# Fifteen small loads of 1 to 15 partitions behind the third load of a streaming log-sum-exp

## The chip, the cores and the metric

The kernel runs on one core of a Trainium2 chip. A core has a matrix engine (PE), a vector engine (DVE), a scalar engine (ACT), a general engine (POOL), a sequencer that issues transfers (SP), and 16 DMA engines that move data between the chip's memory (HBM) and the core's own memory (SBUF, 128 partitions). The metric is the device time of one execution in microseconds. Before the change its median is 161.55 us over two runs (161.54 and 161.56).

## The reference

The input is 32 x 512 rows of 1024 float32 numbers, 64 MiB in all. Each row gives one number, the logarithm of the sum of the exponentials of its elements, made safe by taking the row's maximum out first:

```python
max_x = np.max(x, axis=-1, keepdims=True)
return (max_x.squeeze(-1) + np.log(np.sum(np.exp(x - max_x), axis=-1))).astype(np.float32)
```

The input is drawn from a standard normal distribution, so the output is 16384 float32 numbers, 64 KiB.

## The kernel before

The 16384 rows are laid over 128 partitions, 128 rows on each. The rows stream through `ring`, a buffer of 48 rows (192 KiB) in each partition. Eighteen loads bring them in, all issued by SP in program order. The list `LOADS` gives each one's size in rows for each partition, from 16 at the start to 0.47 at the end, and what is done with the rows. Three loads of 16 rows fill the ring; a fourth begins again at its start, and the function `load` (lines 134 to 141) makes SP wait until the engine that used that place last has counted up its semaphore. The first load is moved ahead of the program's opening barrier by `start_early`. Each load has a semaphore of its own (`landed[i]`), which its transfer raises by 16 when all has arrived.

ACT waits for a load to land and replaces its elements by their exponentials in place, without the maximum (line 228). The sums over rows are made by DVE over whole rows (line 239), or by POOL, which adds the two halves of a row (line 233), and DVE over the halves (line 171), or by DVE with an operation that adds halves and sums in one (line 249). The very last row comes in two pieces whose sums ACT makes itself (line 202). Two logarithms on ACT (lines 268 and 281, with line 279 for the rows in between) and two stores on SP (lines 276 and 285) give the result.

Since the exponentials are taken without the maximum, a check runs beside the work: DVE marks sums that lie outside safe limits, PE adds the marks up, and line 308 makes a truth value of them. If it were false, the branch from line 310 on would compute everything again in the safe form; with this input it is not taken. At the end SP waits until the other engines have passed (line 365) and the first store has landed (line 366), clears the semaphores from `landed[0]` up to, but without, `stored` (line 367), and waits for the second store (line 369).

Nothing plans the order of the work: the program is written out, each engine follows its own list, and counters (`Counted`) carry the waits. SP's list in the first part is thus load 1, load 2, load 3, then a wait for DVE's sum over load 1, then load 4, and so on. All of SP's transfers use one hardware queue, whose work the 16 DMA engines do.

Of the kernel before, what the change touches and what calls it, by code (L numbers as in the profile page):

```python
# [15 lines left out]
RING = 48  # L16
B = 16
LATE = 119

# [31 lines left out]
def kernel(  # L53
# [5 lines left out]
    nc = tc.nc  # L59
# [11 lines left out]
    x_flat = x.flatten_outer_dims()  # L71
# [12 lines left out]
    def source(e0, size):  # L84
        assert e0 >= W * d or e0 + size <= W * d
        return x_rest[:, e0 - W * d : e0 - W * d + size] if e0 >= W * d else x_rows[:, e0 : e0 + size]
# [8 lines left out]
    def sbuf(name, cols, dtype=fp32, rows=P):  # L95
        return nc.alloc_sbuf_tensor(name, [rows, cols], dtype).ap()

    ring = sbuf("ring", RING * d)
    sumexp = sbuf("sumexp", NC)
    res = sbuf("res", NC)  # L100
    clamped = sbuf("clamped", NC)
# [18 lines left out]
    done = nc.alloc_semaphore("done")  # L120
    again = nc.alloc_semaphore("again")
    ready = nc.alloc_semaphore("ready")
    stored = nc.alloc_semaphore("stored")

    nc.scalar.preload_act_table_set("natural_log_exp_and_others")  # L125
# [8 lines left out]
    def load(i, here, done_before, size):  # L134
        for a, b, who, at in users:
            if a < here + size and b > here:
                sp.wait(who, at)
        users[:] = [u for u in users if not (u[0] < here + size and u[1] > here)]
        return nc.sync.dma_start(
            out=ring[:, here : here + size], in_=source(done_before, size)  # L140
        ).then_inc(landed[i], 16)

    def check_early():
        dve.wait(act, summed_by_act)
        dve.wait(dve, dve.n)
        dve.did(nc.vector.tensor_scalar(  # L146
            out=clamped[:, 0:LATE], in0=sumexp[:, 0:LATE],
            scalar1=LOW, scalar2=HIGH, op0=ALU.max, op1=ALU.min,
        ))
        dve.wait(dve, dve.n)  # L150
        dve.did(nc.vector.scalar_tensor_tensor(  # L151
            out=clamped[:, 0:LATE], in0=clamped[:, 0:LATE], scalar=0.0, in1=sumexp[:, 0:LATE],
            op0=ALU.bypass, op1=ALU.not_equal, accum_out=bad[:, 0:1],
        ))
        pe.wait(dve, dve.n)
        pe.did(nc.tensor.matmul(count, lhsT=bad[:, 0:1], rhs=far, start=True, stop=False))  # L156

    def add_up(c, who, **kw):
        pe.wait(*who)
        return pe.did(nc.tensor.matmul(count, lhsT=ones, rhs=sumexp[:, c : c + 1], **kw))  # L160
# [3 lines left out]
    def reduce_folded():  # L164

        nonlocal early_sum
        while folded:
            c0, s0, p0, n0 = folded.pop(0)
            halves = ring[:, p0 : p0 + s0 * d].rearrange("p (c d) -> p c d", d=d)[:, :, 0:H]
            dve.wait(pool, n0)  # L170
            at = dve.did(nc.vector.reduce_sum(  # L171
                out=sumexp[:, c0 : c0 + s0], in_=halves, axis=AX.X
            ))
            users.append((p0, p0 + s0 * d, dve, at))
            if c0 < W:
                early_sum = at
# [9 lines left out]
    for i, (size, ops) in enumerate(loads):  # L186
        if here + size > RING * d:
            assert here == p
            p = here = 0
        if any(q < here + size and q + t * d > here for _, t, q, _ in folded):  # L190
            reduce_folded()
        dma = load(i, here, done_before, size)
        first_load = first_load or dma.ins
        end = here + size
        done_before += size
        act.wait(landed[i], 16)
        for k, (how, s) in enumerate(ops):
            rows = ring[:, p : p + s * d].rearrange("p (c d) -> p c d", d=d)
            if how in "YZ":

                assert c == LAST and (how == "Z" or here == p)
                at = act.did(nc.scalar.activation(  # L202
                    out=last_exp[:, here - p : end - p], in_=ring[:, here:end], func=AF.Exp,
                    accum_out=first_sum if how == "Y" else last_sum,
                ))
                if how == "Z":
                    last_piece = ring[:, here:end]
                here = end
                if how == "Y":
                    nc.vector.addr_align(128, offset=0, max_nops=0)  # L210
                    dve.wait(act, at)
                    first_piece = dve.did(nc.vector.tensor_copy(out=sumexp[:, LAST:NC], in_=first_sum))  # L212
                summed_by_act = at
            elif how == "A":
                assert here == p
                v = ring[:, p : p + d]
                at = act.did(nc.scalar.activation(
                    out=v, in_=v, func=AF.Exp, accum_out=sumexp[:, c : c + 1]
                ))
                here += d  # L220
                users.append((p, p + d, act, at))
                summed_by_act = at
                who = (act, at)
            else:

                upto = end if k + 1 == len(ops) and c + s < LAST else p + s * d
                v = ring[:, here:upto]
                at = act.did(nc.scalar.activation(out=v, in_=v, func=AF.Exp))  # L228
                here = upto
            if how == "F":  # L230
                reduce_folded()
                pool.wait(act, at)
                at = pool.did(nc.gpsimd.tensor_tensor(  # L233
                    out=rows[:, :, 0:H], in0=rows[:, :, 0:H], in1=rows[:, :, H:d], op=ALU.add
                ))
                folded.append((c, s, p, at))
            elif how == "R":
                dve.wait(act, at)
                who = (dve, dve.did(nc.vector.reduce_sum(  # L239
                    out=sumexp[:, c : c + s], in_=rows, axis=AX.X  # L240
                )))
                users.append((p, p + s * d, *who))
            elif how == "T":
                if c >= W:
                    reduce_folded()
                dve.wait(act, at)
                for r in range(s):
                    lo = rows[:, r, 0:H]
                    who = (dve, dve.did(nc.vector.scalar_tensor_tensor(  # L249
                        out=lo, in0=lo, scalar=1.0, in1=rows[:, r, H:d],  # L250
                        op0=ALU.mult, op1=ALU.add, accum_out=sumexp[:, c + r : c + r + 1],
                    )))
                    users.append((p + r * d, p + (r + 1) * d, *who))
                    if c + r >= LATE:
                        add_up(c + r, who, start=False, stop=False)
            if how == "A" and c >= LATE:
                add_up(c, who, start=False, stop=False)
            if how in "RT":
                if c < W:
                    early_sum = dve.n  # L260
                reduce_folded()
            c += s
            p += s * d
            if c == LATE:

                act.wait(dve, early_sum)
                act.wait(act, early_act)
                ln_early = act.did(nc.scalar.activation(  # L268
                    out=res[:, 0:W], in_=sumexp[:, 0:W], func=AF.Ln
                ))  # L270
                check_early()
            if c <= W:
                early_act = summed_by_act
        assert here == end
# [7 lines left out]
        out=res[:, LAST:NC], in_=last_sum, func=AF.Ln, bias=sumexp[:, LAST:NC]  # L282
# [7 lines left out]
    dve.did(nc.vector.scalar_tensor_tensor(  # L290
        out=clamped[:, LATE:NC], in0=sumexp[:, LATE:NC], scalar=LOW,
        in1=sumexp[:, LATE:NC], op0=ALU.max, op1=ALU.not_equal, accum_out=bad[:, 1:2],
# [9 lines left out]
        out=over[:, 0:half], in0=last_piece[:, 0:half], scalar=CEILING,  # L302
# [3 lines left out]
    at = pe.did(nc.tensor.matmul(count, lhsT=bad[:, 2:3], rhs=steep, start=False, stop=True))  # L306
    dve.wait(pe, at)
    at = dve.did(nc.vector.tensor_scalar(out=fine, in0=count, scalar1=HIGH, scalar2=None, op0=ALU.is_lt))  # L308
# [10 lines left out]
    with nc.If(all_fine < 1):  # L319
# [5 lines left out]
        for c0 in range(0, NC, RING):  # L325
# [6 lines left out]
            for c1, c2 in ((c0, edge), (edge, c0 + s)):  # L332
                if c1 == c2:
                    continue
                nc.scalar.dma_start(
                    out=ring[:, (c1 - c0) * d : (c2 - c0) * d],
                    in_=source(c1 * d, (c2 - c1) * d),
# [4 lines left out]
                out=neg, in_=v, op=ALU.max, axis=AX.X, negate=True  # L342
# [3 lines left out]
                out=v, in0=v, in1=neg[:, :, None].to_broadcast([P, s, d])  # L346
# [5 lines left out]
                out=sumexp[:, c0 : c0 + s], in_=v, axis=AX.X  # L352
# [11 lines left out]
    nc.scalar.sem_inc(done, 1)  # L364
    nc.sync.wait_ge(done, 2)
    nc.sync.wait_ge(sp.sem, 16)
    nc.sync.sem_clear(range(landed[0].num, stored.num))
    kind = dict(sync_type="semaphore", id=stored.num, ant_name="stored")
    nc.sync.add_instruction(mybir.InstEventSemaphore(
# [53 lines left out]
```

## Time and profile before

| | |
|---|---|
| median of 2 runs | 161.55 us |
| the profiled execution, from first to last instruction (its span) | 160.4 us |
| median less that span | 1.2 us |
| ACT busy, DVE busy, POOL busy | 114.5, 114.3, 37.3 us |
| moved by DMA | 67.18 MB in 2881 packets, 419 GB/s over the span |
| transfers | 18 loads and 2 stores, all issued by SP |

The profile is one execution. Its page gives each engine's busy time, the span cut into 40 slices with a digit for the busy share of each (9 means 90% or more), the DMA queues with packets and bytes, and the chain of work that ended last, followed back from the last instruction. Further views group instructions by line, give each stretch of time its busy sums, and list who waited for whom. "SPq" is SP's list of transfers. The time that is put down to issuing a transfer is SP's own; the time to landing runs from there to the last rise of the transfer's semaphore. Times within the execution count from its first instruction.

### The profile page before, as it was taken

The page shows a single profiled execution, that of the slowest core. Times are in us where ns is not written, and L with a number is a line of the kernel's source. Part 1 is how long each engine was busy: PE and PEld are TensorE (multiplying, and loading weights), DVE is VectorE, ACT ScalarE, POOL GpSimd, SP SyncE. Part 2 cuts the span into 40 slices and gives each one's busy share as a digit, 9 for nine tenths or more (in the row PEclk, how much of TensorE's full clock was granted, in tenths as well). Part 3 has the DMA queues.
Part 4 walks back from the last instruction along what each step waited for, and adds up shares of the span by engine and source line. Part 5 has one row for each costly group of instructions (what it writes and reads, how often), then busy time and mean ns, then how long its engine had stood idle before and what let it go on. Part 6 is the DMA issues. An engine that isn't in the chain of part 4 may idle for free.

```text
span 160.4 us, 219 instructions
## 1 busy us (share of the span) xinstructions
PE 2.2 (1%) x26; PEld 1.1 (1%) x26; DVE 114.3 (71%) x59; ACT 114.5 (71%) x31; POOL 37.3 (23%) x11
## 2 busy tenths in 40 slices
PE   0000000000000000000000000000000000000022
PEld 0000000000000000000000000000000000000011
DVE  0000000009999499994999859959999999999996
ACT  3000059990699708995099949991999989799996
POOL 0000000000000000000000994690004969891000
DMA  7996996996996996996999999999999999999992
GB/s 262 523 523 262 523 523 262 523 507 278 523 490 294 523 490 294 523 490 294 482 441 441 441 425 409 409 409 480 432 395 417 450 416 398 448 411 424 412 413 95
DMA packets 2881, 67.18 MB, mean 419 GB/s; under 512 B 576, under 2 KB 704, under 8 KB 1344
## 3 DMA queue, kind: packets, MB, share of 16 engines
q1 hardware_dynamic: 2880, 67.18, 97.7%
q14 instruction: 1, 0.01, 0.0%
HBM read 67.11 MB, written 0.07 MB: 419 GB/s over the span
## 4 chain that ended last, share of the span: by engine, by line
DMA 52%; ACT 28%; DVE 19%; issue 1%; PE 0%
DMA ring<-in_x_dram 52%; ACT ring L228 27%; DVE sumexp L239 15%; DVE sumexp L171 2%; DVE ring L249 1%; DVE over L301 0%; PE count L306 0%; ACT res L268 0%; DVE clamped L290 0%; DVE fine L308 0%; DVE sumexp L212 0%
## 5 line engine op out<-in xcount | busy, mean ns | idle before, releaser
L228 ACT ACTIVATE ring<-ring 128x16384 f32<-128x16384 f32 (+16 forms) x23 | 111.7, 4908 | 43.0 <-DMA ring<-in_x_dram 43.0
L239 DVE TENSOR_REDUCE sumexp<-ring 128x16 f32<-128x16384 f32 (+4 forms) x9 | 85.6, 9513 | 42.7 <-ACT ring L228 42.7
L233 POOL TENSOR_TENSOR ring<-ring 128x3072 f32<-128x3072 f32 (+3 forms) x7 | 37.1, 5313 | 107.3 <-ACT ring L228 107.3
L171 DVE TENSOR_REDUCE sumexp<-ring 128x6 f32<-128x3072 f32 (+3 forms) x7 | 18.4, 2656 | 0.0
L249 DVE SCALAR_TENSOR_TENSOR ring<-ring 128x512 f32<-128x512 f32 x15 | 9.6, 687 | 0.4 <-ACT ring L228 0.4
L125 ACT ACT_TABLE_LOAD x1 | 1.3, 1283 | 1.4 <-PEq L62 1.4
L156 PE MATMUL count<-far,bad 128*1 128x1 f32 x2 | 0.2, 164 | 153.2 <-DVE clamped L151 153.2
L160 PE MATMUL count<-sumexp,ones 128*1 128x1 f32 x18 | 1.6, 164 | 3.6 <-DVE ring L249 3.6
L249 DVE DVE_READ_ACCUMULATOR ring<-ring 128x1 f32 x15 | 1.2, 82 | 0.0
L202 ACT ACTIVATE last_exp<-ring 128x544 f32<-128x544 f32 (+1 forms) x2 | 1.2, 584 | 0.0
L126 DVE MEMSET ones<- 128x1 f32 x1 | 0.1, 59 | 1.5 <-PEq L62 1.5
L156 PEld LDWEIGHTS count<-far,bad 128*1 128x1 f32 x2 | 0.1, 80 | 153.2 <-DVE clamped L151 153.2
L160 PEld LDWEIGHTS count<-sumexp,ones 128*1 128x1 f32 x18 | 0.8, 80 | 4.5 <-DVE ring L249 4.5
L301 DVE SCALAR_TENSOR_TENSOR over<-ring 128x240 f32<-128x240 f32 x1 | 0.4, 404 | 0.0
L308 DVE TENSOR_SCALAR fine<-count 1x1 int32<-1x1 f32 x1 | 0.1, 147 | 0.3 <-PE count L306 0.3
L151 DVE SCALAR_TENSOR_TENSOR clamped<-clamped,sumexp 128x119 f32<-128x119 f32 x1 | 0.3, 283 | 0.0
L268 ACT ACTIVATE res<-sumexp 128x112 f32<-128x112 f32 x1 | 0.3, 279 | 0.0
L281 ACT ACTIVATE res<-last_sum,sumexp 128x1 f32<-128x1 f32 x1 | 0.3, 261 | 0.0
L202 ACT ACTIVATION_READ_ACCUMULATOR last_exp<-ring 128x1 f32 x2 | 0.3, 126 | 0.0
L146 DVE TENSOR_SCALAR clamped<-sumexp 128x119 f32<-128x119 f32 x1 | 0.2, 221 | 0.0
L279 ACT ACTIVATE res<-sumexp 128x15 f32<-128x15 f32 x1 | 0.2, 209 | 0.0
L290 DVE SCALAR_TENSOR_TENSOR clamped<-sumexp 128x9 f32<-128x9 f32 x1 | 0.2, 169 | 0.0
(17 smaller groups left out, 1.8 us busy)
## 6 DMA issues: line engine op xcount, KB each, us to landing
ring<-in_x_dram SPq DMA_DIRECT2D x1, 6912.0 KB, 23.9
ring<-in_x_dram SPq DMA_DIRECT2D x1, 6400.0 KB, 19.7
ring<-in_x_dram SPq DMA_DIRECT2D x1, 4608.0 KB, 15.9
ring<-in_x_dram SPq DMA_DIRECT2D x1, 3584.0 KB, 24.0
ring<-in_x_dram SPq DMA_DIRECT2D x1, 3072.0 KB, 19.1
ring<-in_x_dram SPq DMA_DIRECT2D x1, 2288.0 KB, 24.1
ring<-in_x_dram SPq DMA_DIRECT2D x1, 1664.0 KB, 20.9
ring<-in_x_dram SPq DMA_DIRECT2D x1, 1264.0 KB, 23.6
```

The source lines that it names most:

```text
L125: nc.scalar.preload_act_table_set("natural_log_exp_and_others")
L151: dve.did(nc.vector.scalar_tensor_tensor(out=clamped[:, 0:LATE], in0=clamped[:, 0:LATE], scalar=0.0, in1=sumexp[:, 0:LATE], op0=ALU.bypass ...
L156: pe.did(nc.tensor.matmul(count, lhsT=bad[:, 0:1], rhs=far, start=True, stop=False))
L160: return pe.did(nc.tensor.matmul(count, lhsT=ones, rhs=sumexp[:, c : c + 1], **kw))
L171: at = dve.did(nc.vector.reduce_sum(out=sumexp[:, c0 : c0 + s0], in_=halves, axis=AX.X))
L202: at = act.did(nc.scalar.activation(out=last_exp[:, here - p : end - p], in_=ring[:, here:end], func=AF.Exp, accum_out=first_sum if how == ...
L228: at = act.did(nc.scalar.activation(out=v, in_=v, func=AF.Exp))
L233: at = pool.did(nc.gpsimd.tensor_tensor(out=rows[:, :, 0:H], in0=rows[:, :, 0:H], in1=rows[:, :, H:d], op=ALU.add))
L239: who = (dve, dve.did(nc.vector.reduce_sum(out=sumexp[:, c : c + s], in_=rows, axis=AX.X)))
L249: who = (dve, dve.did(nc.vector.scalar_tensor_tensor(out=lo, in0=lo, scalar=1.0, in1=rows[:, r, H:d], op0=ALU.mult, op1=ALU.add, accum_out ...
L268: ln_early = act.did(nc.scalar.activation(out=res[:, 0:W], in_=sumexp[:, 0:W], func=AF.Ln))
L301: dve.did(nc.vector.scalar_tensor_tensor(out=over[:, 0:half], in0=last_piece[:, 0:half], scalar=CEILING, in1=last_piece[:, half : 2 * half ...
```

## The change

A buffer `marks` of 512 float32 columns (2 KiB in each partition) is put behind the ring, and a semaphore `marked` before `stored`. Directly after the third load (`i == MARKED`, counted from 0), SP issues fifteen more transfers. The first reads the first 31 numbers of each of the first 15 rows of the input into 15 partitions, the next 30 numbers of 14 rows into 14 partitions, and so on down to 17 numbers of one row into one partition. Each has a place of its own in `marks` and raises `marked` by 16. Nothing reads `marks`. At the end SP waits for `marked` to reach 240 before it clears the semaphores, which now include `marked`.

```diff
+MARKED = 2
...
     ring = sbuf("ring", RING * d)
+    marks = sbuf("marks", 512)
     sumexp = sbuf("sumexp", NC)
...
     ready = nc.alloc_semaphore("ready")
+    marked = nc.alloc_semaphore("marked")
     stored = nc.alloc_semaphore("stored")
...
         dma = load(i, here, done_before, size)
         first_load = first_load or dma.ins
+        if i == MARKED:
+            for k in range(15, 0, -1):
+                at = 32 * k
+                nc.sync.dma_start(
+                    out=marks[0:k, at : at + 16 + k], in_=x_flat[0:k, 0 : 16 + k]
+                ).then_inc(marked, 16)
         end = here + size
...
     nc.sync.wait_ge(sp.sem, 16)
+    nc.sync.wait_ge(marked, 16 * 15)
     nc.sync.sem_clear(range(landed[0].num, stored.num))
```

On SP's list the fifteen transfers stand between the third and the fourth load. The lists of PE, DVE, ACT and POOL hold the same instructions in the same order as before.

## The prediction

> **What bounds the kernel now.** I read the page first: the span, the busy shares, the slices of the DMA engines and the chain.
>
> ```profile
> span 160.4 us, 219 instructions
> ...
> DVE  0000000009999499994999859959999999999996
> ACT  3000059990699708995099949991999989799996
> ...
> DMA  7996996996996996996999999999999999999992
> ...
> q1 hardware_dynamic: 2880, 67.18, 97.7%
> ...
> DMA 52%; ACT 28%; DVE 19%; issue 1%; PE 0%
> ...
> L228 ACT ACTIVATE ring<-ring 128x16384 f32<-128x16384 f32 (+16 forms) x23 | 111.7, 4908 | 43.0 <-DMA ring<-in_x_dram 43.0
> ```
>
> The DMA engines' packets take 97.7% of 16 engines' span, while DVE and ACT have holes until about slice 32. ACT's idle time, 43.0 us, is all put down to loads. The chain gives only 52% to DMA, so I looked at stretches of the span (time, PE, PEld, DVE, ACT and POOL busy, clock, DMA share and GB/s), and then at ACT's first instructions in the timeline.
>
> ```profile
> 60.00:80.00 20.00, 0.00 (x0) 0.00 (x0) 17.87 (x2) 13.86 (x1) 0.00 (x0) 1.00 1.01 437
> ...
> 138.00:150.00 12.00, 0.00 (x0) 0.00 (x0) 12.00 (x12) 11.78 (x5) 6.17 (x3) 1.00 1.00 426
> 150.00:158.00 8.00, 1.51 (x16) 0.69 (x16) 7.51 (x26) 8.00 (x9) 0.00 (x0) 1.00 0.93 373
> ```
>
> ```profile
> 22.00 13.86 ACT L228 ACTIVATE ring<-ring 128x16384 f32<-128x16384 f32 x1 [19.27 <-DMA ring<-in_x_dram]
> ...
> 41.33 13.86 ACT L228 ACTIVATE ring<-ring 128x16384 f32<-128x16384 f32 x1 [5.46 <-DMA ring<-in_x_dram]
> ...
> 60.68 13.86 ACT L228 ACTIVATE ring<-ring 128x16384 f32<-128x16384 f32 x1 [5.49 <-DMA ring<-in_x_dram]
> ...
> 80.02 13.95 ACT L228 ACTIVATE ring<-ring 128x9216 f32<-128x9216 f32 x2 [5.49 <-DMA ring<-in_x_dram]
> ```
>
> The first loads land every 19.3 us (41.33 less 22.00, 60.68 less 41.33), and ACT needs 13.9 us for each, so it waits 5.5 us each time. A load of 16 rows is 8.39 MB, which over 19.34 us is 434 GB/s. The DMA share stays near 1.0, so the queue of loads never runs dry. The chain in order of time shows where this stops:
>
> ```profile
> 72.46 23.87 DMA ring<-in_x_dram
> ...
> 119.11 19.09 DMA ring<-in_x_dram
> 138.20 0.02 issue
> 138.22 12.34 ACT ring L228 x5
> ```
>
> Its DMA pieces run from a load's issue to its landing. The fifth load is issued at 72.46, but the one ahead of it lands only at 80.02, so the issue is 7.6 us early, and the DVE sum in front of it binds nothing. From 138.20 on, when the ninth load lands, ACT works without a gap to the end (8.00 of 8.00 us in the last stretch). So the end is set by the landing of the ninth load, which the uninterrupted stream of loads sets. **Whatever delays that stream behind the third load, on the DMA engine that finishes a load last, comes out at the end in full.** What delays SP within its slack costs nothing.
>
> **The change part by part.** First SP. Its timeline shows the third load's issue at 1.83, merged with the fourth, whose issue has a row of its own; the next rows are SP's waits and the issue's duration (minimum, median, maximum in ns).
>
> ```profile
> 1.83 51.64 SPq L139 DMA_DIRECT2D ring<-in_x_dram  x2
> ...
> 53.14 0.33 SPq L139 DMA_DIRECT2D ring<-in_x_dram  x1
> ...
> SPq L139 <- DVE sumexp L239: 95.5, 4, 50.8
> ...
> SPq L367 <- ACTq L364: 0.7, 1, 0.7
> ...
> L139 SPq DMA_DIRECT2D ring<-in_x_dram x18: 327/410/2217, 0.0 to 137.0; - x18
> ```
>
> The fifteen issues cost 15 x 0.41 = 6.2 us by the median and 33 us by the longest. They lie in the 50.8 us in which SP waits for DVE before the fourth load, so they cost nothing at the end. With that cover gone, the fourth load could still come late by 60.68 - 53.14 = 7.5 us, while the third is moving.
>
> The added wait for `marked` stands where SP waits 0.7 us for ACT's last step anyway. The marks have landed some 90 us earlier by any case below but one. I take 0. Without that cover it is one more semaphore step of SP, some hundredths of a microsecond. The 2 KiB that move `sumexp` and the later buffers add no instruction to any compute engine: 0.
>
> Now the DMA engines. The queue had 2880 packets: 20 transfers x (128 rows + 16 rises of the semaphore). So a load leaves 8 rows and one rise on each engine. The marks add 15 + 14 + ... + 1 = 120 packets of 68 to 124 bytes, and 120 to 240 rises. Their bytes, 120 x 124 at most, are 15 KB or 0.03 us of the stream; what counts is the price of a packet. No row of before shows a small read, so I bound it by the two nearest rows. The first is the last store, 128 packets of 64 bytes and 16 rises in 0.4 us; the second is the last full microsecond of small loads.
>
> ```profile
> DMA packets 144, 0.01 MB, mean 21 GB/s; under 512 B 144, under 2 KB 144, under 8 KB 144
> ...
> q1 hardware_dynamic: 144, 0.01, 23.1%
> ```
>
> ```profile
> DMA packets 221, 0.41 MB, mean 409 GB/s; under 512 B 23, under 2 KB 120, under 8 KB 221
> ...
> q1 hardware_dynamic: 221, 0.41, 105.6%
> ```
>
> The store: 0.231 x 0.4 us x 16 / 144 = 10.3 ns a packet. The small loads: 1.056 x 1 us x 16 / 221 = 76 ns a packet, where packets are reads from HBM but are some 20 to 40 times larger. The worst-placed engine gets one packet and one rise of each mark, 30 packets: **0.31 us** by the first row, 2.3 us by the second. I take the first, since its packets have the size of the marks, and keep 2.3 us as the upper end. The lower end is 0: the engines don't finish a load together. This is the stretch from 59.7 to 60.4 us, where each engine goes over from the third load to the fourth, in slices of 17.5 ns:
>
> ```profile
> GB/s 0 0 0 3745 0 7490 0 0 3745 3745 0 0 3745 3745 3745 0 0 7490 3745 0 3745 7490 0 0 0 0 0 0 0 0 0 3745 0 0 3745 0 0 0 0 0
> DMA packets 32, 1.05 MB, mean 1498 GB/s; under 512 B 16, under 2 KB 16, under 8 KB 16
> ```
>
> Sixteen new rows start from the 4th to the 35th slice, 0.54 us apart, and the last two come 0.18 us behind the fourteen others. A delay of 0.31 us on an engine among the first is hidden behind the last one; on one of the last two it counts in full. Below nothing: if the marks held up only early engines and took contention from the late ones, the gain is at most the 0.54 us by which the last engine trails.
>
> [...]
>
> **The sum.** Profiled span 160.4 + 0 (SP) + 0 (end wait) + 0.31 = 160.7 us. The median lies 1.15 us above the span, which I leave: 161.9 us. The term itself is uncertain by more than its place, so this first case spans 161.3 to 162.2.
>
> **The rivals.** *Small reads are dear.* Each mark waits in part for its read, and packets go at up to 76 ns. Then the time is 161.55 + up to 2.3 = 163.8, still no change by 2%. For it: the trace has no read under 1920 bytes. Against it: loads of 2 to 3 KB rows keep the stream at 409 GB/s, so reads lie one behind the other without waiting.
>
> *SP is held, and the stream of loads breaks.* This is the one that ends on the other side. Here are the last load's issue, and times to landing of some transfers.
>
> ```profile
> 137.02 2.22 SPq L139 DMA_DIRECT2D ring<-in_x_dram  x1
> ```
>
> ```profile
> ring<-in_x_dram SPq DMA_DIRECT2D x1, 3072.0 KB, 19.1
> ring<-in_x_dram SPq DMA_DIRECT2D x1, 2288.0 KB, 24.1
> ...
> ring<-in_x_dram SPq DMA_DIRECT2D x1, 240.0 KB, 20.9
> ...
> out_dram<-res SPq DMA_DIRECT2D x1, 8.0 KB, 1.4
> ```
>
> At 137.02 the ninth to the seventeenth load had been issued and not landed (the ninth, of 3072 KB, lands at 138.20). The issue of the eighteenth took 2.22 us where others take 0.41. So there is a limit. If it is nine transfers in flight, then behind three loads SP gets six marks out; the seventh waits for load 1 (22.0), the eighth for load 2 (41.3), the ninth for load 3 (60.7). Seven more issues of 0.41 us bring the fourth load's to 63.5, not 53.14. The DMA engines then stand still from 60.7 until about 1 us after that issue (the store of 8 KB lands 1.4 us after its own), 4 to 5 us, and all that follows comes so much later: 166 us, between 165 and 167. It decides once more than nine transfers may not be in flight. Against it: the long issue ended at 139.24, one microsecond after the ninth load had landed, so its landing isn't what released it. Room for packets fits better. The tenth load (2288 KB) lands at 143.6, so its eight rows take 0.68 us each, and at 139.24 the slowest engine was on its second. It then held about 8 x 9 - 1 packets and the new 9, some 80. Three loads and the marks are 27 + 30 = 57, less than that. [...]
>
> *Marks one after the other.* If each had to land before the next began, each costs up to the store's 1.4 us: 15 x 1.4 = 21 us, 182.6 us. Against it: the 240 KB load was issued with eight or nine ahead and landed with the stream at 157.9, without a gap of that kind between the small loads (409 GB/s over that microsecond). [...]
>
> *The marks even the engines out*: at best 0.54 us less, 161.0.
>
> **How the numbers follow.** The first case, packets at about the store's price, has 0.60; dear small reads (162.2 to 163.8) 0.20; SP held (165 to 167) 0.12; marks in series (above 168) 0.05; engines evened out 0.02; anything faster by over 2% 0.01, since at the 434 GB/s of the first loads the 67.1 MB need 154.6 us, the last load lands 2.5 us before the span's end (157.9) and 1.15 us lie outside it, 158.3 us even without a start. Two per cent, 3.2 us, is about what a measurement of this kernel can tell from no change. So faster 0.01, same 0.82, slower 0.17. The range takes the first two cases, 0.80 together: 161.3 to 163.9.
>
> **What would show it.** In the profile after: 3120 to 3240 packets on the queue; fifteen issues of 0.3 to 0.5 us between 2.3 and 10 us; the fourth load still issued at about 53.1; ACT's third start at 60.7 as before, its fourth 0 to 0.4 us after 80.02; the same shift at 138.2. A fourth load issued after 60, or a hole in the DMA slices near slice 15, means that SP was held. A shift at ACT's fourth start that is over 0.5 us with SP on time means dear small reads. The prediction is wrong if the shift grows after the fourth load, where nothing was changed.

## The result and the profile after

The changed kernel takes 163.18 us (163.16 and 163.19) where the kernel before takes 161.55 us: a ratio of 1.0096, 95% interval 1.0078 to 1.0115. By 2% that is no change, yet it is 1.63 us more, clear of the spread of the runs, and five times the 0.31 us that the sum had for it. In the experiments below, the kernel before ran again with medians of 161.64 to 161.70 us, and the ratios there are against these.

First the page of the changed kernel.

```profile
span 161.9 us, 234 instructions
...
DVE  0000000019999499985999649969999999999996
ACT  3000059980899609994089958991999989799996
...
DMA  8996996997998996998999999998999999999991
...
DMA packets 3122, 67.20 MB, mean 415 GB/s; under 512 B 817, under 2 KB 945, under 8 KB 1585
## 3 DMA queue, kind: packets, MB, share of 16 engines
q1 hardware_dynamic: 3120, 67.19, 97.4%
...
L237 ACT ACTIVATE ring<-ring 128x16384 f32<-128x16384 f32 (+16 forms) x23 | 111.7, 4908 | 44.4 <-DMA ring<-in_x_dram 44.4
```

The span grew by 1.5 us and ACT's wait for loads by 1.4 us; its busy time did not move. The queue has 240 packets more: in the trace 120 rows of 68 to 124 bytes and 120 rises of 4 bytes. They stand in chains, a mark's row, its rise, then the next mark: one engine has six marks, from 124 down to 104 bytes, ahead of the fourth load's row that it begins at 59.77, another only the first two ahead of its row at 60.23. The only row of 68 bytes, that of the last mark, starts at 60.055, and the large row that begins 0.012 us later takes 4.05 us, the longest of the sixteen. So the trace agrees with one row and one rise on each of k engines for a mark of k rows, and with one engine that gets all fifteen marks.

Next the timeline: SP's transfers, and ACT's instructions that wait for the third, the fourth and the ninth load.

```profile
2.37 5.47 SPq L200 DMA_DIRECT2D marks<-in_x_dram  x15
53.06 87.13 SPq L142 DMA_DIRECT2D ring<-in_x_dram  x15
...
60.61 13.86 ACT L237 ACTIVATE ring<-ring 128x16384 f32<-128x16384 f32 x1 [5.50 <-DMA ring<-in_x_dram]
81.45 13.95 ACT L237 ACTIVATE ring<-ring 128x9216 f32<-128x9216 f32 x2 [6.99 <-DMA ring<-in_x_dram]
...
139.66 12.36 ACT L237 ACTIVATE ring<-ring 128x2048 f32<-128x2048 f32 x5 [1.03 <-DMA ring<-in_x_dram]
```

SP issued the marks by 7.84 and the fourth load on time. From the third load's landing to the fourth's it is now 81.45 - 60.61 = 20.84 us, before 80.02 - 60.68 = 19.34. **The whole 1.50 us is lost there**, and it stays: from the third load to the ninth it is 79.05 us, before 77.54, 1.51 more. I use this step from third to fourth landing below, since a different start of the execution drops out of it.

The DMA engines show how. This is the stretch from 79 to 83 us in slices of 0.1 us, in which the engines go over from the fourth load to the fifth: first the kernel before, then the changed one.

```profile
GB/s 553 1659 2212 2765 553 553 553 0 0 0 0 0 0 0 0 0 0 0 0 0 0 1659 2212 2212 1659 0 1106 0 0 0 0 0 0 0 0 0 0 0 0 0
```

```profile
GB/s 0 0 0 0 0 1106 2212 1106 0 0 553 0 553 0 553 1106 0 553 0 0 1106 0 0 0 0 553 1106 2212 553 0 553 0 0 553 553 1106 0 0 553 0
```

Each packet counts in the slice in which it starts, and 553 GB/s is one row of 55 KB in 0.1 us. Before, all sixteen engines begin the fifth load's first row within 0.7 us. After, half begin it within 0.3 us of one another and the rest come later, the last 1.5 us after the first. The engines were held by different amounts, and none makes it up again.

### The profile page after: what moved, and what is told of

The parts are those of the page before. It is cut to its first block, busy times and chain, and to the rows that moved or that the text cites. A ratio compares the mean times of both kernels' runs of the same rounds, so it can differ in the third digit from the quotient of the medians.

```text
span 161.9 us, 234 instructions
## 1 busy us (share of the span) xinstructions
PE 2.2 (1%) x26; PEld 1.1 (1%) x26; DVE 114.3 (71%) x59; ACT 114.5 (71%) x31; POOL 37.3 (23%) x11
## 4 chain that ended last, share of the span: by engine, by line
DMA 52%; ACT 27%; DVE 18%; issue 1%; PE 0%
DMA ring<-in_x_dram 52%; ACT ring L237 27%; DVE sumexp L248 15%; DVE sumexp L174 2%; DVE ring L258 1%; DVE over L310 0%; PE count L315 0%; ACT res L277 0%; DVE clamped L299 0%; DVE fine L317 0%; DVE sumexp L221 0%
```

## The experiments

**Which engines, how many packets, and what they read.** After the result I had a theory: an engine fetches only so many packets ahead, the thirty small ones on the worst-placed engine use that up, and the fourth load's first row is then fetched late. The rivals were a price for each transfer, one for each small row, and dear small reads from HBM. Four kernels changed the marks alone. Every diff is against the changed kernel, except two that say otherwise. Where the number of marks changes, so does the count that SP waits for at the end; that line is left out.

```diff
-                    out=marks[0:k, at : at + 16 + k], in_=x_flat[0:k, 0 : 16 + k]
+                    out=marks[0:1, at : at + 17], in_=x_flat[0:1, 0:17]
```

> Edit: fifteen marks of one row of 17 numbers each, in place of 15 to 1 rows. If the delay is that of the worst-placed engine, whose 30 small packets keep the next load's first row from being fetched ahead (theory: read-ahead), the 15 packets and 15 rises all fall on one engine as before and the time stays where the change put it, 163.0 to 163.3 us. If the price goes with the number of small rows in all (120 before, 15 now), it falls to an eighth, 161.6 to 161.8 us.

Measured: 163.35 us, ratio 1.0108 (1.0091 to 1.0125). One engine with fifteen marks costs as much as the change does; the change's 105 further rows on other engines add nothing that shows.

```diff
-            for k in range(15, 0, -1):
+            for k in range(15, 8, -1):
```

> Edit: only the first seven marks, of 15 to 9 rows. The worst-placed engines get 14 small packets. Read-ahead: in the trace after the change the engines with seven marks or fewer fetched the next row at most 0.36 us late, so the time is 161.6 to 162.1 us. A price for each transfer, in proportion (7 of 15 of 1.63 us): 162.3 us.

Measured: 162.15 us, ratio 1.0033 (1.0019 to 1.0047), between the two expectations.

```diff
-            for k in range(15, 0, -1):
+            for k in range(3):
...
-                    out=marks[0:k, at : at + 16 + k], in_=x_flat[0:k, 0 : 16 + k]
+                    out=marks[:, at : at + 17], in_=x_flat[0:P, 0:17]
```

> Edit: three marks of 128 rows of 17 numbers in place of the fifteen. Each engine gets 3 x (8 + 1) = 27 small packets. Read-ahead counts packets: 162.8 to 163.3 us, all engines late alike. A price for each transfer counts three of fifteen: 161.9 us.

Measured: 161.92 us, ratio 1.0022 (1.0011 to 1.0032). The theory fell here. The packets of the queue, and ACT's third and fourth start in this kernel:

```profile
q1 hardware_dynamic: 3312, 67.20, 97.9%
```

```profile
60.56 13.86 ACT L237 ACTIVATE ring<-ring 128x16384 f32<-128x16384 f32 x1 [5.61 <-DMA ring<-in_x_dram]
80.04 13.95 ACT L237 ACTIVATE ring<-ring 128x9216 f32<-128x9216 f32 x2 [5.63 <-DMA ring<-in_x_dram]
```

It has 432 packets more than before, 27 on every engine, and the step is 19.48 us, only 0.14 us longer. (The trace loses another 0.27 us from the fifth load's landing to the sixth's, where no mark stands; why is not known.) So small packets are cheap here; what this kernel has few of is transfers, and with them rises of the semaphore: three for each engine.

```diff
+    seed = sbuf("seed", 32)
...
+    seeded = dve.did(nc.vector.memset(seed, 1.0))
...
+            sp.wait(dve, seeded)
...
-                    out=marks[0:k, at : at + 16 + k], in_=x_flat[0:k, 0 : 16 + k]
+                    out=marks[0:k, at : at + 16 + k], in_=seed[0:k, 0 : 16 + k]
```

> Edit: the fifteen marks copy from a small buffer in SBUF that DVE has filled at the start, not from HBM. Read-ahead: what comes late is the next load's row, not the mark, so nothing changes, 163.0 to 163.3 us. If small reads from HBM are dear themselves: 161.6 to 162.0 us.

Measured: 163.22 us, ratio 1.0095 (1.0078 to 1.0112). The change, with its reads from HBM, took 163.18: reading from HBM is not what costs.

**How the price grows.** Two theories were left: A, that rises pass one after the other, each at a price; B, that an engine looks ahead over a few transfers only, and the next load pays one fetch. They differ where there are more marks.

```diff
-            for k in range(15, 0, -1):
-                at = 32 * k
+            for k in range(30):
+                at = 17 * k
...
-                    out=marks[0:k, at : at + 16 + k], in_=x_flat[0:k, 0 : 16 + k]
+                    out=marks[0:1, at : at + 17], in_=x_flat[0:1, 0:17]
```

> Edit: thirty marks of one row of 17 numbers, twice the fifteen of the earlier run, all on one engine. Three wide marks (27 small packets, 3 rises of the semaphore on each engine) cost next to nothing, so packets are not what counts; rises or transfers on an engine are. Theory A, each rise waits for the confirmed write of its own mark, one after the other: the price goes on in proportion. Fifteen cost 1.7 us and seven 0.5 us on an engine, 0.15 us for each further one, so thirty cost 1.7 + 15 x 0.15 = 3.9 us: 165.2 to 165.9 us. Theory B, the engine fetches ahead over a few transfers only, and the next load's first row pays one fetch from HBM: that price is paid once, and thirty cost 1.7 to 2.0 us plus 0.2 us for 30 more packets: 163.3 to 163.9 us.

Measured: 166.18 us, ratio 1.0273 (1.0256 to 1.029), A's side and somewhat beyond it. Here are ACT's starts with fifteen single rows, and then with thirty, with SP's issues (minimum, median, maximum in ns).

```profile
60.59 13.86 ACT L237 ACTIVATE ring<-ring 128x16384 f32<-128x16384 f32 x1 [5.49 <-DMA ring<-in_x_dram]
81.71 13.95 ACT L237 ACTIVATE ring<-ring 128x9216 f32<-128x9216 f32 x2 [7.26 <-DMA ring<-in_x_dram]
```

```profile
60.53 13.86 ACT L237 ACTIVATE ring<-ring 128x16384 f32<-128x16384 f32 x1 [5.50 <-DMA ring<-in_x_dram]
84.20 13.95 ACT L237 ACTIVATE ring<-ring 128x9216 f32<-128x9216 f32 x2 [9.81 <-DMA ring<-in_x_dram]
```

```profile
L200 SPq DMA_DIRECT2D marks<-in_x_dram x30: 245/287/7209, 2.4 to 35.7; - x30
```

The step is 21.12 us with fifteen and 23.67 with thirty: 2.55 us for fifteen more, **0.17 us each**. The price goes on in proportion, so B is out. The fourth load was still issued on time, at 52.97. The last row shows something else too: SP was stopped while it issued the marks. The trace has the first 23 issues at 0.25 to 0.35 us each, and from the 24th on, at 9.65, all seven that are left at 2.4 to 7.2 us. By the 24th that engine had been given 27 + 48 = 75 packets, less the few rows that it had done. If it is room for packets that ran out, that room is somewhat under the some 80 of the prediction's count, an estimate from these counts; no run shows the room itself. Fifteen marks, 57 packets, were issued without such a stop.

```diff
-                    out=marks[0:k, at : at + 16 + k], in_=x_flat[0:k, 0 : 16 + k]
+                    out=marks[0:16, at : at + 16 + k], in_=x_flat[0:16, 0 : 16 + k]
```

> Edit: fifteen marks of 16 rows each in place of 15 to 1 rows, so that every engine gets one row and one rise of each. If the worst-placed engine alone sets the end: 163.0 to 163.5 us, as with the change. If the unevenness of the engines is part of the price: 161.9 to 162.6 us.

Measured: 164.48 us, ratio 1.0164 (1.0147 to 1.0181): neither. The step is 83.08 - 60.76 = 22.32 us, 2.98 more than before, where one engine alone with fifteen costs 1.78.

```profile
60.76 13.86 ACT L237 ACTIVATE ring<-ring 128x16384 f32<-128x16384 f32 x1 [5.50 <-DMA ring<-in_x_dram]
83.08 13.95 ACT L237 ACTIVATE ring<-ring 128x9216 f32<-128x9216 f32 x2 [8.46 <-DMA ring<-in_x_dram]
```

So engines that end marks at the same time hindered each other here. In the trace, six of the sixteen begin the fourth load's first row, which stands behind the marks, by 60.82 us and take 3.3 to 4.3 us over it. The other ten begin it only from 61.47 to 63.38, because their marks' own packets pass late; with one marked engine, all had begun it by 60.26. It is not the small reads as such: three wide marks put 24 small reads on every engine, and there all sixteen rows began by 60.27. Where the engines meet was not tried.

**The rises themselves.** In the next kernel each mark has a semaphore of its own, so that the trace shows which mark each rise belongs to.

```diff
-    marked = nc.alloc_semaphore("marked")
+    marked = [nc.alloc_semaphore(f"marked{k}") for k in range(15)]
...
-            for k in range(15, 0, -1):
-                at = 32 * k
+            for k in range(15):
...
-                    out=marks[0:k, at : at + 16 + k], in_=x_flat[0:k, 0 : 16 + k]
-                ).then_inc(marked, 16)
+                    out=marks[k : k + 1, 0:17], in_=x_flat[k : k + 1, 0:17]
+                ).then_inc(marked[k], 16)
...
-    nc.sync.wait_ge(marked, 16 * 15)
+    for each in marked:
+        nc.sync.wait_ge(each, 16)
```

> Edit: fifteen marks of one row of 17 numbers, all on one engine, each into a partition and with a semaphore of its own, so that the profile shows each one's landing. If each rise waits for its own mark's confirmed write before the next mark goes on, the fifteen land one after the other at even steps of 0.15 to 0.2 us (thirty marks cost 2.8 us more than fifteen, 0.19 us for each), some 2.5 us from first to last, although their packets pass within 0.3 us; the time is that of the earlier run with fifteen single rows, 163.0 to 163.6 us. If the marks only keep the next load's row from being fetched: they land within 0.5 us of each other.

Measured: 163.25 us, ratio 1.0098 (1.0078 to 1.0118). The trace's records of the fifteen rises, in us from the span's start:

```
60.354 60.530 60.705 60.880 61.065 61.248 61.429 61.616 61.799 61.980 62.163 62.345 62.537 62.721 62.903
```

They come at even steps of 0.18 us, 2.55 us from first to last. The packets are long past by then. In the kernel with fifteen single rows on one semaphore, this is the stretch from 60.03 to 60.24 us, in which nearly all that starts is the marked engine's small packets, with a peak of 13 or 14 for each of the fourteen marks in it. The large packet at the end is another engine's row; the marked engine's own row starts at 60.26:

```profile
GB/s 0 0 1 13 0 1 13 1 13 0 1 13 0 1 13 1 13 0 1 13 0 1 13 0 14 0 1 13 0 1 13 0 1 13 1 13 0 2 12496 0
DMA packets 30, 0.07 MB, mean 317 GB/s; under 512 B 29, under 2 KB 29, under 8 KB 29
```

29 small packets in about 0.2 us are 7 ns each, less than the 10.3 ns of the prediction's sum. The marks pass in that time, and **their rises follow one after the other at 0.18 us each**. The next load's row ends late by that: in that kernel its packet took 4.11 us instead of 2.42, from 60.26 to 64.37, and it ended 1.23 us after the last rise (63.14). The same 1.23 us stand between the last rise and the end of the row with thirty marks and with own semaphores. So some 1.2 us of a 2.42 us row get done while the rises are still passing, and about that much of their time is hidden: 15 x 0.18 - 1.2 = 1.5 us, 30 x 0.18 - 1.2 = 4.2 us (measured steps: 1.6 to 1.8 and 4.33 us longer than before).

> Edit: the same with seven marks on the one engine. Serial rises take 7 x 0.18 = 1.2 us. Fifteen on one engine take 2.7 us and cost 1.7, thirty take 5.3 us and cost 4.5, so about 1 us of them is hidden, and seven alone on one engine should cost 0.1 to 0.4 us, 161.7 to 162.1 us; seven on nine engines at once cost 0.5 us. If rises of several engines don't hinder each other, the two cost the same.

The same kernel with `range(7)` and seven semaphores measured 161.80 us, ratio 1.0007 (0.9998 to 1.0017): no difference that can be told. The trace shows that the row does not hide all seven: it took 2.79 us instead of 2.42, from 59.74 to 62.53, and again ended 1.23 us after the last rise (61.30). These 0.37 us, two rises, don't show, since this engine was not behind the others: a row on an engine without marks ended at 62.55. So the row hid about five rises, and the engine's lead the rest. The seven marks of 15 to 9 rows cost 0.5 us. By the chains of the changed kernel they stand on nine engines at once, where rows took up to 3.05 us, 0.63 more than 2.42 and 0.26 more than the 2.79 of the one engine with seven, so these engines too hindered each other, and engines that trail can be among them. What each of the two adds was not told apart.

**What a rise waits for.** I had taken it that a rise waits until its mark's write is confirmed. Two kernels changed that write; their diffs are against the kernel with fifteen semaphores.

```diff
-                    out=marks[k : k + 1, 0:17], in_=x_flat[k : k + 1, 0:17]
+                    out=marks[k : k + 1, 0:509], in_=x_flat[k : k + 1, 0:509]
```

> Edit: fifteen marks of one row of 509 numbers (2036 bytes, 0.075 us of an engine at its share of 434 GB/s) on one engine. If the next mark's write goes on while a rise waits, the bytes lie inside the waits and the steps between landings stay 0.15 to 0.2 us: 163.0 to 163.8 us. If write and wait follow each other, the steps grow by 0.075 to some 0.25 us and the time by 1.1 us: 164.2 to 164.8 us.

Measured: 163.66 us, ratio 1.0123 (1.0103 to 1.0143). Thirty times the bytes cost 0.4 us more, not 1.1: from the fifth on, the rises again stand 0.18 us apart (63.231 - 61.413 over ten steps), and the bytes pass inside the waits.

```diff
+    seed = sbuf("seed", 32)
+    aside = nc.dram_tensor("aside", [16, 1024], fp32, kind="Internal").ap()
...
-                    out=marks[k : k + 1, 0:17], in_=x_flat[k : k + 1, 0:17]
+                    out=aside[k : k + 1, 0:17], in_=seed[k : k + 1, 0:17]
```

> Edit: fifteen marks of one row of 17 numbers on one engine that are written from SBUF to a scratch tensor in HBM. If the step is the wait for the mark's write to be confirmed, it changes with the place that is written: a longer step than 0.18 us and a later end, above 163.6 us. If the step is a fixed price of a rise, it stays 0.18 us and the time 163.0 to 163.6 us.

Measured: 163.21 us, ratio 1.0096 (1.0075 to 1.0116), steps of 0.18 us (60.277 to 62.823 over fourteen). Whether the mark goes to SBUF or to HBM, these steps are the same. So 0.18 us is a price of a mark's end on its engine, and not, as far as these runs tell, the wait for the place that the mark writes. No run tells the rise from the rest of the transfer that it ends. From the third load's landing to the fourth's it is 20.79 us here, 1.45 more than before, where the two kernels that read fifteen marks of 17 numbers from HBM on one engine lose 1.6 and 1.8. The marked engine's own row took much the same in all three (4.09 to 4.16 us); the rest I put down to how far that engine was ahead of the others.

**Other places for the marks.**

```diff
-        if i == MARKED:
-            for k in range(15, 0, -1):
...
+        for k in {2: (15, 9, 3), 3: (14, 8, 2), 4: (13, 7, 1), 5: (12, 6), 6: (11, 5), 7: (10, 4)}.get(i, ()):
```

> Edit: the same fifteen marks, in groups of two or three behind the third to the eighth load. Theories A and B both let the first three or so of a group be hidden behind the rows of the load: 161.6 to 162.0 us. A fixed price for each mark wherever it stands: 163.0 to 163.3 us.

Measured: 162.31 us (161.78 to 162.55 over ten runs), ratio 1.0032 (1.0021 to 1.0043): a third of the price, but more than expected.

```profile
60.77 13.86 ACT L236 ACTIVATE ring<-ring 128x16384 f32<-128x16384 f32 x1 [5.50 <-DMA ring<-in_x_dram]
80.13 13.95 ACT L236 ACTIVATE ring<-ring 128x9216 f32<-128x9216 f32 x2 [5.50 <-DMA ring<-in_x_dram]
...
138.97 12.41 ACT L236 ACTIVATE ring<-ring 128x2048 f32<-128x2048 f32 x5 [1.48 <-DMA ring<-in_x_dram]
```

The first group of three is free (a step of 19.36 us, before 19.34), as the theory says. From the third load to the ninth it is 78.20 us, 0.66 more than before, and 0.44 of that come with the last group, of only two marks (the eighth to the ninth load: 7.75 us, before 7.31). The rows behind that group are 24 KB and may hide less, which no run measured, but two rises of 0.18 us do not make 0.44. On the engine that ends last, the trace has the second mark start 0.25 us after the first was through (131.00, after 130.76), and then a row of 1.22 us where most take 0.91. Why that mark started late stays open.

```diff
-                nc.sync.dma_start(
+                nc.scalar.dma_start(
```

> Edit: the same fifteen marks, issued by ACT between its second and third exponential, so that they go through a queue of their own beside the loads. If the loads' queue is held only by what stands in it: 161.5 to 161.9 us, since ACT has 5.5 us of idle time there for some 5 us of issues. If an engine is held whatever the queue: 163 us.

Measured: 162.65 us (161.96 to 163.4 over ten runs), ratio 1.0063 (1.0046 to 1.008). On a queue of their own the marks are not free either, and the times differ more from run to run than those of any other kernel here.

```profile
41.52 5.66 ACTq L200 DMA_DIRECT2D marks<-in_x_dram  x15
60.88 13.86 ACT L237 ACTIVATE ring<-ring 128x16384 f32<-128x16384 f32 x1 [5.51 <-DMA ring<-in_x_dram]
80.31 13.95 ACT L237 ACTIVATE ring<-ring 128x9216 f32<-128x9216 f32 x2 [5.57 <-DMA ring<-in_x_dram]
```

The profiled execution is one of the short ones (span 160.8 us): ACT's issues lie beside its second exponential, and the step is 19.43 us, 0.09 longer. The trace has single rises of the marks as late as 104 us. They come in groups, at first 4.9 us apart (48, 53, 58 us), the time of two rows, as if the two queues took turns. What the longer runs lose was not seen in a profile. None of these kernels is faster than the one before.

## Why the prediction was right, and where its sum was not

- **The bound.** Right. The end follows the landing of the ninth load, which the stream sets: 1.50 us lost between the third and the fourth load, 1.51 at the ninth, 1.5 in the span.
- **SP.** Right. The fifteen issues took 5.47 us (6.2 expected) inside the 50.8 us of waiting, the fourth load was issued at 53.06, and the last wait cost nothing. The rival in which SP is held at nine transfers in flight is out: eighteen were in flight at 7.84.
- **The DMA engines.** The step that failed. "I take the first, since its packets have the size of the marks": 30 packets at 10.3 ns, 0.31 us. The packets passed even faster, at 7 ns. What the sum left out is that fifteen rises stand close together on one engine. It counted a rise as a packet like any other, from a store that has one rise for eight rows. No row of before shows how the rows and rises of a mark are dealt out to the engines, so the thirty packets on one engine and the 120 rises, the lower end of the count, were my estimate; the trace after has 120 rises, and its chains agree with fifteen marks on one engine. In its place stand 15 x 0.18 us less the 1.2 us that the next row hides, about 1.5 us. So the first case, 161.3 to 162.2 at 0.60, was missed.
- **The rivals.** The time came out in the band of dear small reads (162.2 to 163.8, at 0.20), but small reads were not dear: marks from SBUF cost the same (163.22 us, the change 163.18), and three wide marks made the step 0.14 us longer. That this band made the range wide enough was luck. The prediction's sign for this rival, a shift of over 0.5 us at ACT's fourth start with SP on time, came (1.4 us), and would have led to the wrong cause. Nearest in mechanism was the rival with marks one after the other, at 0.05. It priced a mark at up to 1.4 us, where it is 0.18, and I argued against it with small loads that land without gaps. These stand at least 0.6 us apart, the time of eight rows of 1920 bytes, so a step of 0.18 us could not show there.
- **The forecast** of no change by 2%, and the range of 161.3 to 163.9, held; the likeliest time of 161.9 was 1.3 us short.

## What to carry to other kernels

In a stream that the DMA engines bound, count the transfers that end on each engine one right after the other, not only bytes and packets: each such end took 0.18 us here, and a long row behind them hid about the first five on one engine. Three transfers over all 128 partitions, 384 small rows, made the next load 0.14 us later; fifteen of one row each, all on one engine, made it 1.8 us later. What one engine lost, the others did not make up: in the changed kernel the sixteen engines' rises for the fourth load stand from 79.88 to 81.43 us, ACT began at 81.45, and the 1.50 us lost there were 1.51 at the ninth load.

## What was not expected of the hardware

Transfers that end one right behind the other on one DMA engine raised their semaphores 0.18 us apart, although their packets passed in 7 ns each. The step was the same 0.18 us for marks of 68 and, from the fifth rise on, of 2036 bytes from HBM to SBUF, and for marks of 68 bytes from SBUF to HBM. The row of 64 KB behind them, 2.42 us long without marks, ended 1.23 us after the last rise. Fifteen marks on all sixteen engines made the next load land 2.98 us later, on one engine alone 1.45 to 1.78. And the 0.54 us by which engines stood apart in the kernel before became 1.5 us in the changed kernel and stayed between 1.5 and 1.6 to the last load.
